# A macaron decoder layer on one core: inputs handed over in the layout in which the kernel reads them

## The chip, the cores and the metric

One core of a Trainium2 chip runs the whole layer in one launch. The metric is the device time of one execution in microseconds (us); the figure of a kernel is the median over its runs. A profile is of one further execution, with its own time.

## The reference, cut to what matters

Input `x` is (1, 256, 2048) float32, all weights are float32, and there is one layer:

```python
x = x + 0.5 * swiglu(rms_norm(x, ffn1_norm), w1, w3, w2)       # (silu(x@w1) * (x@w3)) @ w2, width 5632
h = rms_norm(x, mix_norm); proj = h @ w_in                     # columns q|k, v, o, i, f, u (4104)
y = concat[ mLSTM heads (4, chunkwise, conv on q|k) | S5 groups (64 groups of 16 channels, state 64) ]
x = x + y @ w_out                                              # S5: states by B, scan, out by C, gelu, GLU
x = x + 0.5 * swiglu(rms_norm(x, ffn2_norm), ...)
out = rms_norm(x, final_norm)
```

In the S5 part, each group's states are read out by `real(states * C)`, with `C = c_re + i c_im` of shape (64, 16, 64), and `d_skip` is a factor per channel.

## The kernel before, in words

**Products in three parts.** TensorE gets float32 numbers as two float32r parts, `hi` and `lo`, and forms `xh*wh + xl*wh + xh*wl`. Each weight is used once. The weights come in *steps*: a step is two k-tiles of 128 rows by 512 columns, 512 KB. `fetch` (L151) issues the load on SP's queue (`wraw`, 4 buffers), ScalarE casts it to `whi` (L157), and VectorE subtracts to `wlo` (L159; 4 buffers each). `plan` (L107) lists all steps in the order of use, and `weights` (L143) keeps three steps fetched ahead. `step_tok` (L162) is one step of a product with tokens on rows: 8 matmuls with `whi`, then 4 with `wlo`, 512 columns each.

**Activations with channels on rows.** The left operand needs channels on the partitions. `x` is loaded with tokens on partitions in four pieces of 512 columns (`load_x`, L257), and `transpose_x` (L329) turns one piece by 8 transposes on TensorE (L341), from whose PSUM result ScalarE writes `xh` (times the norm's gain, L346) and VectorE `xl` (L351). The norm's factor per token (`rstd`) is applied after the product, from sums of squares of `x` (`sumsq`, L325).

**The start.** `start` (L189) is the first product (w1, columns 0 to 511, 8 steps, called M0 to M7 here). Its order on PE, ACT and DVE is written out by hand: piece 0 of `x` is turned, then weight steps and the turning of pieces 1 to 3 alternate, with the sums of squares behind steps 4 to 7. Dummy matmuls (`warm`, L308: 8 and then 4) stand ahead of the first product. All DMAs on SP stand in program order; on the other engines a planner orders what isn't written out by hand.

**Vectors.** Norm gains, conv weights and the like are rows of 128 in HBM. `ffn1_norm` is loaded first and turned on TensorE (L272); the other 96 rows come by seven DMAs on POOL's queue (L287), are turned at the 6th step behind the start (L294) and copied to `cols`.

**Background tasks.** While the first FFN runs, each step's end (`tick`, L83) lets tasks of `s5_params` (L508) go, at about 0.42 per step: parameters of the S5 part are loaded by POOL's queue and, for each of 8 blocks `j`, tables are built and written back to HBM (`spill`, L762). For C, both parts are loaded with channels on rows (`craw`, L538), masked to two groups on VectorE (`stage_c`, L718), turned by two transposes on TensorE (L734) and copied to `w2` by ScalarE, the second with a minus sign (L735, L736). `clam` (L740) and `kzero` (L750) read `w2`.

**The end.** `tail` (L415) does the last 512 columns in two halves of 256, with loads of its own (L427).

Of the kernel before, what the change touches and what calls it, by code (L numbers as in the profile page):

```python
# [8 lines left out]
F32 = mybir.dt.float32  # L9
F32R = mybir.dt.float32r  # L10
# [30 lines left out]
WARM = 8  # L41
MORE_WARM = 4
# [20 lines left out]
class _Layer:  # L63
# [87 lines left out]
    def fetch(self, name, k, kk, c0, n):  # L151
        nc = self.nc
        view = self.wview(name)
        raw = self.wraw.tile([P, KK * NC], F32, name="wraw")[:, :kk * n]
        nc.sync.dma_start(out=raw.rearrange("p (k n) -> p k n", n=n), in_=view[:, k:k + kk, c0:c0 + n])
        hi = self.whi.tile([P, KK * NC], F32R, name="whi")[:, :kk * n]
        nc.scalar.copy(hi, raw)  # L157
        lo = self.wlo.tile([P, KK * NC], F32R, name="wlo")[:, :kk * n]
        nc.vector.tensor_sub(lo, raw, hi.bitcast(F32))  # L159
        return hi.rearrange("p (k n) -> p k n", n=n), lo.rearrange("p (k n) -> p k n", n=n)  # L160
# [28 lines left out]
    def start(self, acc, view, gain):  # L189

        W = lambda i: self.weights(view, i * KK, KK, 0, NC)
        M = lambda i, w: self.step_tok(acc, self.xs, [(i * KK, 0), (i * KK + 1, 0)], w, NC, i == 0, i == 7)
        T = lambda c, halves=(0, 1): self.transpose_x(c, gain, halves)
        ET = mybir.EngineType
        with self.tc.manual_schedule(engines={ET.PE, ET.Activation, ET.DVE}):
            self.load_x(0)
            T(0, (0,))
            self.ahead.append((self.steps[0], self.fetch(*self.steps.pop(0))))
            T(0, (1,))
            self.warm(MORE_WARM)  # L200
            self.ahead.append((self.steps[0], self.fetch(*self.steps.pop(0))))
            self.load_x(1)
            for i in range(8):
                M(i, W(i))
                if i % 2 == 0 and i < 6:
                    T(i // 2 + 1)
                if i % 2 == 0 and i < 4:
                    self.load_x(i // 2 + 2)
                if i >= 4:
                    self.sumsq(i - 4)  # L210
        self.finish_rstd()
# [22 lines left out]
    def wview(self, name):  # L234
        return self.a[name][0].rearrange("(k p) n -> p k n", p=P)


    def setup(self):
# [16 lines left out]
        vec0 = self.s5p.tile([KD, P], F32, name="vec0", tag="s5k0")  # L255
        nc.sync.dma_start(out=vec0, in_=self.a["ffn1_norm"][0].rearrange("(k p) -> k p", p=P))
# [13 lines left out]
        self.cols0 = c.tile([P, KD], F32, name="cols0")  # L270
        b = self.bank()
        nc.tensor.transpose(b[:, :KD], vec0, self.ident[:KD, :KD])  # L272
        nc.vector.tensor_copy(self.cols0, b[:, :KD])
        rows = 16 + 16 + 32 + 8 * 4
        vecs = self.s5p.tile([rows, P], F32, name="vecs", tag="s5k0")
        r = 0
        where = {}
        for name, n in (("mix_norm", 16), ("ffn2_norm", 16), ("conv_w", 32), ("conv_b", 8), ("mlstm_norm", 8),
                        ("d_skip", 8), ("b_glu", 8)):
            src = self.a[name][0]  # L280
            if name == "conv_w":
                src = src.rearrange("w (j p) -> (w j) p", p=P)
            elif name == "d_skip":
                src = src.rearrange("(j r) h -> j (r h)", r=8)
            else:
                src = src.rearrange("(k p) -> k p", p=P)
            nc.gpsimd.dma_start(out=vecs[r:r + n, :], in_=src)  # L287
            where[name] = r
            r += n
        self.cols = c.tile([P, rows], F32, name="cols")  # L290

        def late():
            b = self.bank()
            nc.tensor.transpose(b[:, :rows], vecs, self.ident[:rows, :rows])  # L294
            nc.vector.tensor_copy(self.cols, b[:, :rows])
            w = where["b_glu"]
            nc.vector.tensor_scalar(self.cols[:, w:w + 8], self.cols[:, w:w + 8], 0.5, None, op0=ALU.mult)
            w = where["mlstm_norm"]
            nc.vector.tensor_scalar(self.cols[:, w:w + 8], self.cols[:, w:w + 8], 0.5, None, op0=ALU.mult)
# [3 lines left out]
        nc.vector.memset(self.gcol, 0.0)  # L303
        for i, name in enumerate(("b_i", "b_f")):
            nc.gpsimd.dma_start(out=self.gcol[32 * i:32 * i + H, :], in_=self.a[name][0].rearrange("(h o) -> h o", o=1))
# [62 lines left out]
    def ffn(self, l, chunk_done):  # L368
        nc = self.nc
        w1, w3, w2 = (f"ffn{l}_{n}" for n in ("w1", "w3", "w2"))  # L370
        with ExitStack() as ctx:
# [4 lines left out]
            for hi_, n in enumerate(HALVES):  # L376
                gs = []
                self.rate = self.ffn1_rate if l == 1 else 1
                for c in range(n):
                    cc = c0 + c  # L380
                    ks = [(k, k) for k in range(KD)]
                    p1 = self.pair()
                    if l == 1 and cc == 0:
                        self.start(p1, w1, lambda k: self.cols0[:, k:k + 1])
                    else:
                        self.gemm_tok(p1, self.xs, w1, ks, cc * NC, NC)
                    s = []
                    for t in range(TT):
                        s.append(fp.tile([P, NC], F32, name=f"s{t}"))
                        nc.scalar.activation(s[t], p1[t], AF.Silu, scale=self.rstd[:, t:t + 1])  # L390
# [24 lines left out]
    def tail(self, w2, gs, c0):  # L415
# [6 lines left out]
        for half in range(2):  # L422
            col = c * NC + half * W
            ws = []
            for i, k0 in enumerate(range(0, n, 4)):
                raw = self.wraw.tile([P, KK * NC], F32, name="wraw")
                nc.sync.dma_start(out=raw.rearrange("p (k n) -> p k n", n=W),  # L427
                                  in_=self.wview(w2)[:, c0 * 4 + k0:c0 * 4 + k0 + 4, col:col + W])
# [79 lines left out]
    def s5_params(self, ctx):  # L508
# [13 lines left out]
        craw = [sp.tile([P, NJ, 64], F32, name=f"craw{i}") for i in range(2)]  # L522
# [6 lines left out]
        load(out=self.wgr, in_=self.wview("w_in")[:, :, GATE0:GATE0 + 2 * H])  # L529
# [7 lines left out]
        for i, nm in enumerate(("c_re", "c_im")):  # L537
            load(out=craw[i], in_=self.a[nm][0].rearrange("(j r) h p -> (r h) j p", r=8))  # L538
# [4 lines left out]
        maskg = sp.tile([P, 2], F32, name="maskg")  # L543
        maskq = sp.tile([P, 4], F32, name="maskq")

        def layout():
# [11 lines left out]
            V.tensor_reduce(maskg, self.ident.rearrange("p (q g h) -> p g q h", q=4, g=2), op=ALU.add, axis=AX.XY)  # L558
# [130 lines left out]
        def per_j(j):  # L689
# [26 lines left out]
            stc = [st.tile([P, 2, 64], F32, name=f"stc{ri}") for ri in range(2)]  # L716
# [520 lines left out]
```

## Time and profile before

| | |
|---|---|
| median of 3 runs | 1839.52 us (1839.28 to 1840.48) |
| the profiled execution | 1839.91 us, its span 1838.2 us |
| PE (TensorE) busy | 1821.5 us, 99% |
| DVE (VectorE) busy | 1064.4 us, 58% |
| ACT (ScalarE) busy | 818.1 us, 45% |
| POOL (GpSimd) busy | 348.9 us, 19% |
| read from HBM | 344.6 MB, mean 195 GB/s with all else |

Busy time of an engine is what its instructions cover. Matmuls overlap each other in the records, so the step from one start to the next tells more than a duration. "Idle before" is the time that an engine stood before an instruction, with what ended it.

### The profile page before, as it was taken

Reading aid. Unit: us, or ns where it says so; the run is one execution under the profiler, and the core shown is the slowest. Engines: PE = TensorE matmul, PEld = TensorE weight load, DVE = VectorE, ACT = ScalarE, POOL = GpSimd, SP = SyncE. Lnnn points to the kernel's source line nnn. Section 1 sums busy time; section 2 is a strip of 40 time slices with the busy share of each in tenths; the row PEclk is TensorE's granted clock in tenths of the full one; section 3 lists DMA queues with packets and bytes.
Section 4 is the critical chain, followed back from the end, with each engine's and each line's share of the span. In section 5 each row is a group of like instructions: output and inputs, shape, how many; then the busy total and the mean of one; then the engine's idle time right before and its main releaser. Section 6 shows DMA issues by size and latency. Waiting matters only on the chain.

```text
span 1838.2 us, 24018 instructions
## 1 busy us (share of the span) xinstructions
PE 1821.5 (99%) x9174; PEld 1527.0 (83%) x9174; DVE 1064.4 (58%) x1261; ACT 818.1 (45%) x982; POOL 348.9 (19%) x519
## 2 busy tenths in 40 slices
PE   9999999999999999999999999999999999999998
PEld 7888888888888888998977988888888888888887
DVE  5546855555555555578888665454544545454554
ACT  6444444334444445444454564444443334444343
POOL 4000799920000000065545100000000000000011
PEclk9999999999999999999999999999999999999999
DMA  8666676676666665767784556666665666666563
GB/s 275 196 186 185 192 217 214 213 242 196 196 197 195 188 198 195 198 181 208 184 211 149 190 189 201 193 192 189 189 187 192 193 194 191 189 193 186 193 193 128
DMA packets 185652, 358.26 MB, mean 195 GB/s; under 512 B 12064, under 2 KB 18336, under 8 KB 185408
## 3 DMA queue, kind: packets, MB, share of 16 engines
q1 hardware_dynamic: 181344, 344.51, 63.1%
q0 software_dynamic: 4048, 11.16, 1.7%
q8 instruction: 72, 1.18, 0.3%
q10 hardware_dynamic: 144, 1.05, 0.1%
q14 instruction: 44, 0.36, 0.1%
HBM read 344.61 MB, written 11.01 MB: 193 GB/s over the span
## 4 chain that ended last, share of the span: by engine, by line
PE 95%; DVE 2%; DMA 2%; issue 1%; ACT 0%; ACTq 0%; POOLq 0%; POOL 0%; SPq 0%; DVEq 0%
PE accb L177 84%; PE accb L225 2%; PE accb L231 2%; PE accb L226 2%; DVE wlo L159 1%; PE tpb L492 1%; DMA wraw<-in_w_in_dram 1%; PE tpb L341 0%; DMA wraw<-in_ffn_w_dram 0%; PE tpb L852 0%; PE accb L482 0%; PE accb L481 0%; PE accb L480 0%; PE tpb L891 0%; PE tpb L928 0%
## 5 line engine op out<-in xcount | busy, mean ns | idle before, releaser
L159 DVE TENSOR_TENSOR wlo<-wraw,whi 128x1024 fp32r<-128x1024 f32 x622 | 791.1, 1274 | 677.4 <-ACT whi L157 676.8
L157 ACT CAST whi<-wraw 128x1024 fp32r<-128x1024 f32 x622 | 654.4, 1053 | 885.3 <-PE accb L177 814.4
L177 PE MATMUL accb<-whi,xh 128*128 128x512 f32 x1536 | 603.5, 393 | 0.6 <-ACT whi L157 0.6
L177 PE MATMUL accb<-whi,xl 128*128 128x512 f32 x1536 | 598.9, 390 | 0.8 <-DVE xl L351 0.8
L177 PE MATMUL accb<-wlo,xh 128*128 128x512 f32 x1536 | 410.7, 389 | 0.0
L177 PEld LDWEIGHTS accb<-whi,xh 128*128 128x128 f32 x1536 | 289.0, 188 | 61.6 <-ACT whi L157 1.3
L177 PEld LDWEIGHTS accb<-whi,xl 128*128 128x128 f32 x1536 | 289.0, 188 | 60.3 <-DVE xl L351 1.6
L177 PEld LDWEIGHTS accb<-wlo,xh 128*128 128x128 f32 x1536 | 288.3, 188 | 60.1
L177 PE MATMUL accb<-whi,gh 128*128 128x512 f32 x664 | 259.8, 391 | 0.0
L177 PE MATMUL accb<-whi,gl 128*128 128x512 f32 x664 | 258.4, 389 | 0.0
L177 PE MATMUL accb<-wlo,gh 128*128 128x512 f32 x664 | 177.5, 389 | 0.0
L177 PEld LDWEIGHTS accb<-wlo,gh 128*128 128x128 f32 x664 | 124.6, 188 | 25.9
L177 PEld LDWEIGHTS accb<-whi,gh 128*128 128x128 f32 x664 | 124.6, 188 | 25.6
L177 PEld LDWEIGHTS accb<-whi,gl 128*128 128x128 f32 x664 | 124.7, 188 | 25.5
L1201 POOL TENSOR_TENSOR x<-x,fn 128x512 f32<-128x512 f32 x6 | 12.1, 2041 | 689.9 <-ACT junk L323 689.9
L703 POOL TENSOR_TENSOR tr<-s5rot,sp 128x128 f32<-128x128 f32 (+6 forms) x112 | 55.5, 496 | 160.2 <-DVE sp L643 156.7
L225 PE MATMUL accb<-xh,whi 128*128 128x256 f32 x256 | 63.5, 286 | 0.0
L226 PE MATMUL accb<-xl,whi 128*128 128x256 f32 x256 | 62.8, 283 | 0.0
L705 POOL TENSOR_TENSOR s5rot<-tr,tr 128x128 f32<-128x128 f32 (+6 forms) x112 | 61.0, 557 | 3.3
L704 POOL TENSOR_TENSOR tr<-s5rot,sp 128x128 f32<-128x128 f32 (+6 forms) x112 | 57.2, 511 | 0.0
L764 POOL DMA_DIRECT2D spillw<-s5w x16 | 8.6, 541 | 249.6 <-ACT s5w L735 239.2
L225 PEld LDWEIGHTS accb<-xh,whi 128*128 128x128 f32 x256 | 49.1, 192 | 0.8 <-issue 0.4
(316 smaller groups left out, 1345.5 us busy)
## 6 DMA issues: line engine op xcount, KB each, us to landing
wraw<-in_ffn_w_dram SPq DMA_DIRECT2D x528, 512.0 KB, 3.8
wraw<-in_w_in_dram SPq DMA_DIRECT2D x64, 512.0 KB, 5.7
wraw<-in_w_out_dram SPq DMA_DIRECT2D x32, 512.0 KB, 4.2
spillrot<-s5rot POOLq DMA_DIRECT2D x8, 512.0 KB, 5.4
spillw<-s5w POOLq DMA_DIRECT2D x16, 256.0 KB, 4.6
s5rot<-spillrot SPq DMA_DIRECT2D x8, 512.0 KB, 6.9
s5w<-spillw SPq DMA_DIRECT2D x16, 256.0 KB, 7.1
wraw<-in_w_glu_dram SPq DMA_DIRECT2D x8, 512.0 KB, 3.7
```

Of the source, the lines that this page charges most:

```text
L157: nc.scalar.copy(hi, raw)
L159: nc.vector.tensor_sub(lo, raw, hi.bitcast(F32))
L177: nc.tensor.matmul(acc[t][:, :n], lhsT=x, rhs=wt, start=first and t not in seen, stop=last and t not in left)
L225: nc.tensor.matmul(o(nt), lhsT=wh[:, kk, ns(nt)], rhs=xh, start=st, stop=False, **kw)
L226: nc.tensor.matmul(o(nt), lhsT=wh[:, kk, ns(nt)], rhs=xl, start=False, stop=False, **kw)
L231: nc.tensor.matmul(o(nt), lhsT=wl[:, kk, ns(nt)], rhs=xh, start=False, stop=sp, **kw)
L492: nc.tensor.transpose(b[:, o:o + P], s[t][:, kt * P:(kt + 1) * P], self.ident)
L703: G.tensor_tensor(tr[0][:, :, :k], rv[:, 0, :, 0:k], u0, op=ALU.mult)
L704: G.tensor_tensor(tr[1][:, :, :k], rv[:, 1, :, 0:k], u1, op=ALU.mult)
L705: G.tensor_tensor(rv[:, a, :, k:2 * k], tr[0][:, :, :k], tr[1][:, :, :k], op=op)
L764: nc.gpsimd.dma_start(out=d, in_=t)
L1201: nc.gpsimd.tensor_tensor(self.x[c][:, t, :], self.x[c][:, t, :], self.fn[:, c * NC:(c + 1) * NC], op=ALU.mult)
```

## The change

Host-side `_layout` hands the inputs over in other layouts; the kernel's arithmetic stays the same.

- `xT`: x with channels on rows (128 x 16 x 256), beside `x` itself. `start` loads `xT` in place of `x` and splits it straight from SBUF with 256-column instructions; the 32 transposes of L341 in the start go. `x` is loaded at steps 4 to 7; its sums of squares move to the ticks of the second product, and the first Silu (L390) runs at that product's 4th tick.
- `cols`: all 112 vectors with channels on rows in one DMA, the first on SP's queue. The transposes L272 and L294 and POOL's seven loads go; `gcol` is one load in place of two.
- `cT`: C turned and masked on the host. `stage_c` becomes two DMAs on POOL's queue per block straight into `w2`; the mask, the two transposes (L734) and the copy L735 go; the minus sign is a ScalarE instruction in place.
- Weights: every step lies in HBM as one block, 4 KB for each partition, instead of two rows of 2 KB (tail: one of 4 KB instead of four of 1 KB). The first step's load is cut into two DMAs, and its casts into two halves each.
- `warm` is 9 dummy matmuls once, instead of 8 and 4.

```diff
-WARM = 8
-MORE_WARM = 4
+WARM = 9
+    def load(self, name, k, kk, c0, n, parts=1):
+        raw = self.wraw.tile([P, KK * NC], F32, name="wraw")[:, :kk * n].rearrange("p (k n) -> p k n", n=n)
+        m = kk // parts
+        for i in range(0, kk, m):
+            self.nc.sync.dma_start(out=raw[:, i:i + m, :], in_=self.wview(name, k, c0)[:, i:i + m, :])
+        return raw
...
+        def split_x(k):
+            c, i = divmod(k, 4)
+            g = self.col("ffn1_norm", k)
+            nc.scalar.activation(self.xh[c][:, i, :], raw[c][:, i, :], AF.Copy, scale=g)
+            nc.vector.scalar_tensor_tensor(self.xl[c][:, i, :], raw[c][:, i, :], g, self.xh[c][:, i, :].bitcast(F32),
+                                           op0=ALU.mult, op1=ALU.subtract)
+        def prepare(i):
+            step, wr = w[i]
+            if i == 0:
+                tiles = self.split_tiles()
+                for kk in range(KK):
+                    split_x(kk)
+                    ready.append((step, self.split(wr, tiles, slice(kk, kk + 1))))
+                ready.pop()
+                return
+            if i < 8:
+                for kk in range(KK):
+                    split_x(i * KK + kk)
+            ready.append((step, self.split(wr)))
         with self.tc.manual_schedule(engines={ET.PE, ET.Activation, ET.DVE}):
-            self.load_x(0)
-            T(0, (0,))
-            self.ahead.append((self.steps[0], self.fetch(*self.steps.pop(0))))
...
+            load_xT(0, 0, 2)
+            load(0, KK)
+            load_xT(0, 2, 4)
+            load(1)
+            prepare(0)
+            load_xT(1)
+            load(2)
+            prepare(1)
+            load_xT(2)
+            load(3)
             for i in range(8):
-                M(i, W(i))
...
+                prepare(i + 2)
+                if i == 0:
+                    load_xT(3)
+                if i + 4 < 10:
+                    load(i + 4)
                 if i >= 4:
-                    self.sumsq(i - 4)
-        self.finish_rstd()
+                    self.load_x(i - 4)
+                self.step_tok(acc, self.xs, [(i * KK, 0), (i * KK + 1, 0)], ready.pop(0)[1], NC, i == 0, i == 7)
+        self.ahead = ready
...
             def stage_c():
                 for ri in range(2):
-                    src = craw[ri][:, j, :].unsqueeze(1).broadcast_to([P, 2, 64])
-                    self.tc.keep_in_program_order(V.tensor_tensor(
-                        stc[ri], src, maskg.unsqueeze(2).broadcast_to([P, 2, 64]), op=ALU.mult))
+                    nc.gpsimd.dma_start(out=w2[:, ri * P:(ri + 1) * P], in_=self.a["cT"][ri, :, j, :])
...
-                b2 = self.bank()
-                for ri in range(2):
-                    nc.tensor.transpose(b2[:, ri * P:(ri + 1) * P], stc[ri].rearrange("p g q -> p (g q)"), self.ident)
-                nc.scalar.copy(w2[:, 0:128], b2[:, 0:128])
-                nc.scalar.activation(w2[:, 128:256], b2[:, 128:256], AF.Copy, scale=-1.0)
+                nc.scalar.activation(w2[:, 128:256], w2[:, 128:256], AF.Copy, scale=-1.0)
```

## Rows read from the trace of the kernel before

**Rows 1.** The page: busy time and share of each engine

```profile
PE 1821.5 (99%) x9174; PEld 1527.0 (83%) x9174; DVE 1064.4 (58%) x1261; ACT 818.1 (45%) x982; POOL 348.9 (19%) x519
```

**Rows 2.** The page: chain of work that ended last, shares by engine

```profile
PE 95%; DVE 2%; DMA 2%; issue 1%; ACT 0%; ACTq 0%; POOLq 0%; POOL 0%; SPq 0%; DVEq 0%
```

**Rows 3.** Waits: engine, line, releaser, total us, times, longest us

```profile
PE tpb L991 <- DVE Dm L966: 2.6, 1, 2.6
PE accb L177 <- DVE hml L1030: 2.2, 1, 2.2
...
ACT whi L157 <- PE accb L177: 814.4, 517, 2.8
...
ACT whi L157 <- DMA wraw<-in_w_in_dram: 20.9, 12, 3.6
```

**Rows 4.** Timeline of PE: start us, duration us, line, tiles

```profile
1.52 3.59 PE L312 MATMUL tpb<-junk 128*128 128x512 bf16 x8 [1.52 <-DVE junk L260]
5.97 1.09 PE L341 MATMUL tpb<-ident,x 128*128 128x128 f32 x8 [0.69 <-DMA x<-in_x_dram]
...
8.49 0.50 PE L177 MATMUL accb<-whi,xh 128*128 128x512 f32 x1 [0.57 <-ACT whi L157]
...
22.96 0.50 PE L177 MATMUL accb<-whi,xl 128*128 128x512 f32 x1 [0.79 <-DVE xl L351]
...
25.59 1.03 PE L341 MATMUL tpb<-ident,x 128*128 128x128 f32 x8
26.38 0.48 PE L177 MATMUL accb<-whi,xh 128*128 128x512 f32 x1
...
34.63 0.39 PE L177 MATMUL accb<-whi,xh 128*128 128x512 f32 x1
...
37.35 0.39 PE L177 MATMUL accb<-whi,xh 128*128 128x512 f32 x1
...
50.96 0.25 PE L294 MATMUL tpb<-ident,vecs 96*128 96x96 f32 x1
50.99 0.48 PE L177 MATMUL accb<-whi,xh 128*128 128x512 f32 x1
```

**Rows 5.** Chain of waits in order of time: start us, duration us, what

```profile
1.25 4.67 DMA x<-in_x_dram
```

**Rows 6.** Timeline of ACT in the start

```profile
6.67 0.84 ACT L346 ACTIVATE xh<-tpb,cols 128x256 fp32r<-128x256 f32 x2 [4.37 <-PE tpb L341]
7.40 1.04 ACT L157 CAST whi<-wraw 128x1024 fp32r<-128x1024 f32 x1
...
11.38 1.04 ACT L157 CAST whi<-wraw 128x1024 fp32r<-128x1024 f32 x1 [1.26 <-DMA wraw<-in_ffn_w_dram]
12.64 1.05 ACT L157 CAST whi<-wraw 128x1024 fp32r<-128x1024 f32 x1 [0.21 <-DMA wraw<-in_ffn_w_dram]
```

**Rows 7.** Windows: stretch, length, busy of PE PEld DVE ACT POOL, PEclk, DMA, GB/s

```profile
0.00:5.00 5.00, 3.48 (x8) 1.03 (x8) 0.93 (x5) 1.49 (x2) 3.92 (x13) 1.00 0.48 120
5.00:12.00 7.00, 5.75 (x32) 4.31 (x32) 4.58 (x9) 4.07 (x7) 5.10 (x8) 1.00 1.04 394
12.00:18.00 6.00, 5.96 (x28) 4.62 (x27) 4.02 (x6) 2.95 (x6) 0.04 (x1) 1.00 1.04 281
18.00:26.00 8.00, 7.21 (x37) 5.66 (x36) 5.25 (x7) 5.67 (x8) 4.41 (x5) 1.00 0.96 322
26.00:36.00 10.00, 10.00 (x49) 8.35 (x48) 6.47 (x8) 9.68 (x22) 3.74 (x8) 1.00 0.88 243
36.00:44.00 8.00, 8.00 (x37) 6.64 (x36) 4.71 (x6) 6.41 (x9) 1.80 (x1) 1.00 0.81 275
950.00:955.00 5.00, 2.43 (x9) 1.56 (x8) 5.00 (x6) 1.75 (x3) 1.23 (x1) 0.90 1.01 255
955.00:960.00 5.00, 5.00 (x18) 3.88 (x16) 1.93 (x4) 2.34 (x7) 0.00 (x0) 0.76 0.91 295
```

**Rows 8.** Timeline of PE: the transposes of one S5 block

```profile
254.88 0.60 PE L730 MATMUL tpb<-ident,stg 128*128 128x128 f32 x4
255.32 0.38 PE L734 MATMUL tpb<-ident,stc 128*128 128x128 f32 x2
255.46 0.48 PE L177 MATMUL accb<-whi,xh 128*128 128x512 f32 x1
```

**Rows 9.** DMA issues: queue, count, KB each, median us from issue to landing

```profile
craw<-in_c_im_dram POOLq DMA_DIRECT2D x1, 256.0 KB, 6.0
```

More of the change, by code (lines that the diff above doesn't have):

```diff
@@ L149, in weights, with fetch, split_tiles, split @@
         return w
-    def fetch(self, name, k, kk, c0, n):
-        nc = self.nc
[L153 to L160, printed above, removed]
+    def fetch(self, *step):
+        return self.split(self.load(*step))
+    def load(self, name, k, kk, c0, n, parts=1):
[4 more added lines that the diff above has]
+        return raw
+    def split_tiles(self):
+        return (self.whi.tile([P, KK * NC], F32R, name="whi"), self.wlo.tile([P, KK * NC], F32R, name="wlo"))
+    def split(self, raw, tiles=None, ks=None):
+        nc = self.nc
+        kk, n = raw.shape[1:]
+        hi, lo = (t[:, :kk * n].rearrange("p (k n) -> p k n", n=n) for t in tiles or self.split_tiles())
+        ks = ks or slice(0, kk)
+        nc.scalar.copy(hi[:, ks, :], raw[:, ks, :])
+        nc.vector.tensor_sub(lo[:, ks, :], raw[:, ks, :], hi[:, ks, :].bitcast(F32))
+        return hi, lo
     def step_tok(self, acc, xs, part, w, n, first, last):
@@ L187, in gemm_tok, with start, load_xT, load @@
             self.tick()
[L189 to L193, printed above, removed]
+    def start(self, acc, gp):
+        nc = self.nc
         ET = mybir.EngineType
-        with self.tc.manual_schedule(engines={ET.PE, ET.Activation, ET.DVE}):
-            self.load_x(0)
-            T(0, (0,))
-            self.ahead.append((self.steps[0], self.fetch(*self.steps.pop(0))))
[L199 to L202, printed above, removed]
-            for i in range(8):
-                M(i, W(i))
[L205 to L208, printed above, removed]
+        raw = [gp.tile([P, 4, S], F32R, name="gl").bitcast(F32) for c in range(4)]
+        self.xh = [self.xTp.tile([P, 4, S], F32R, name=f"xh{c}") for c in range(4)]
+        self.xl = [self.xTp.tile([P, 4, S], F32R, name=f"xl{c}") for c in range(4)]
+        w, ready = {}, []
+        def load_xT(c, a=0, b=4):
+            nc.sync.dma_start(out=raw[c][:, a:b, :], in_=self.a["xT"][:, 4 * c + a:4 * c + b, :])
+        def load(i, parts=1):
+            w[i] = self.steps.pop(0)
+            w[i] = w[i], self.load(*w[i], parts=parts)
+        def split_x(k):
[17 more added lines that the diff above has]
+            ready.append((step, self.split(wr)))
+        with self.tc.manual_schedule(engines={ET.PE, ET.Activation, ET.DVE}):
+            load_xT(0, 0, 2)
[8 more added lines that the diff above has]
+            load(3)
+            for i in range(8):
+                prepare(i + 2)
[3 more added lines that the diff above has]
+                    load(i + 4)
@@ L254, in setup @@
         xin = self.a["x"][0].rearrange("(t p) n -> p t n", p=P)
-        vec0 = self.s5p.tile([KD, P], F32, name="vec0", tag="s5k0")
-        nc.sync.dma_start(out=vec0, in_=self.a["ffn1_norm"][0].rearrange("(k p) -> k p", p=P))
+        rows = sum(n for _, n in _COLS)
+        self.cols = c.tile([P, rows], F32, name="cols")
+        nc.sync.dma_start(out=self.cols, in_=self.a["cols"])
         self.load_x = lambda i, a=0, b=NC: nc.sync.dma_start(out=self.x[i][:, :, a:b],
@@ L269, in setup @@
         nc.vector.memset(self.mhalf, -0.5)
[L270 to L287, printed above, removed]
+        where, r = {}, 0
+        for name, n in _COLS:
             where[name] = r
             r += n
-        self.cols = c.tile([P, rows], F32, name="cols")
         def late():
[L293 to L299, printed above, removed]
+            for name in ("b_glu", "mlstm_norm"):
+                w = where[name]
+                nc.vector.tensor_scalar(self.cols[:, w:w + 8], self.cols[:, w:w + 8], 0.5, None, op0=ALU.mult)
         self.after(6, late)
@@ L302, in setup @@
         self.gcol = c.tile([GW, 1], F32, name="gcol")
-        nc.vector.memset(self.gcol, 0.0)
-        for i, name in enumerate(("b_i", "b_f")):
-            nc.gpsimd.dma_start(out=self.gcol[32 * i:32 * i + H, :], in_=self.a[name][0].rearrange("(h o) -> h o", o=1))
+        nc.gpsimd.dma_start(out=self.gcol, in_=self.a["gcol"])
         self.wgr = c.tile([P, KD, 2 * H], F32, name="wgr")
@@ L1227 @@
     arrays, args = {}, {}
-    for name in _INS:
-        v = _np.ascontiguousarray(inputs[name])
+    for name, v in _layout(inputs).items():
+        v = _np.ascontiguousarray(v)
         arrays[f"in_{name}_dram"] = v
```

61 lines of the change are left out of this document (46 added, 15 removed).

## The prediction, written before the change was run

> **What bounds the kernel now.** I read the page's busy shares first, then the chain of waits, then who waits for whom, and only then the places that the change touches. TensorE is busy 1821.5 of 1838.2 us [rows 1], and 95% of the chain that ends last is its own work [rows 2]. So only two kinds of time can be won: TensorE instructions that go away, and the few microseconds in which it stands. In mid-kernel it stands about 5 us, in the mixer, and both large waits there end on VectorE (2.6 and 2.2 us), not on a transfer [rows 3]. ScalarE's casts, which follow each weight load, wait 814.4 us for TensorE to free a buffer and only 20.9 us for the mixer's loads [rows 3]: weights normally arrive early. The remaining loss is at the front. The first real matmul starts at 8.49, and M8, the ninth weight step, at 34.63 [rows 4]. A step is 37.35 - 34.63 = 2.72 us, twelve matmuls of 0.227 [rows 4], so eight steps need 21.8 us, and 34.63 - 8.49 = 26.1 were used.
>
> **The start, transposes.** Three turnings of x stand in that stream (the first is ahead of it); the third takes 26.38 - 25.59 = 0.79 from its start to the next matmul [rows 4], so 2.4 of TensorE's work go; they are part of the 4.4 below, as the transfers decide how much of it is seen. The turning of the 96 vectors at 50.96 [rows 4] goes too: a transpose takes 0.79/8 = 0.10, so **0.1**.
>
> **The start, transfers.** These decide where the rest lands, so I count bytes. In the kernel before, 0.60 MB had moved by 5.0 (120 GB/s), then 394 GB/s to 12.0, when 3.36 MB had moved, then 281, 322, 243 and 275 GB/s in the next four stretches [rows 7]. The piece x0 landed at 1.25 + 4.67 = 5.92 [rows 5], when 0.96 MB had moved, though itself and what was ahead of it were 0.53. The load for the cast at 11.38 [rows 6] had 2.63 MB in and ahead of it, and 3.10 had moved; for the one at 12.64 it was 3.15 and 3.53. So a load lands when some 0.43 MB more than itself and its predecessors has moved. In the new order the sums are, in MB: cols 0.06, first half of xT0 0.32, first half of w0 0.58, second half of w0 0.84, w1 1.63, w2 2.68, w3 3.73, w4 4.78, w5 5.30, w8 6.87, then pieces of x between, so w9 7.92, w10 8.97, w11 10.02, w12 11.07.
> By that, half of w0 lands at 5 + (0.58 + 0.43 - 0.60)/0.394 = 6.04. ScalarE has split the first k-tile of xT by then (0.42, half of the 0.84 of two such instructions [rows 6]) and casts half a step, 0.55 of the 1.04 [rows 6]: M0 starts at 6.65 instead of 8.49. VectorE's parts, 0.44 and 0.66 by the same halving, end in time for matmuls 2 and 9. M0 ends at 9.4. w1 lands at 8.71, its cast ends at 9.8, a wait of 0.4: M1 runs to 12.55. w2 lands at 11.37, cast 12.47: no wait, M2 runs to 15.27. From here two bounds. If the queue keeps 394 GB/s, w3 lands at 14.0 and w4 at 16.7, M4 starts at 18.0 with no further wait and M8 at 28.9: 5.7 us gained. If the rates stay those of before at the same times, w3 lands at 14.85 (M3 at 15.95), w4 at 18.5 (M4 at 19.6, waited 0.9), M8 starts at 30.5, and the extra 2.1 MB of x between w8 and w12 bring w12 to 41.3, M12 starts at 42.4 where it was 34.63 + 4 x 2.72 = 45.5: 3.1 gained. I take the middle, **4.4**, because the parameter loads on POOL's queue that stood beside those stretches still run, but the channel-vector loads and the strided gate columns are gone from them. ScalarE keeps up: from M8 on it has a cast of 1.05 and two squares a step, as it had before.
>
> **S5's C.** Two of six transposes of each block go. The six take 255.46 - 254.88 = 0.58 from start to the next matmul, so two are 0.19 to 0.22 [rows 8]; times 8 blocks 1.5 to **1.75**. I take 1.75, as each is a 0.11 slot in a stream that never stands there. The copy on ScalarE and the masks on VectorE go too and cost or give nothing: ScalarE is idle half the time behind TensorE [rows 1, 3]. The new waits: the minus sign on ScalarE, `clam` on VectorE and `kzero` on TensorE now wait for a DMA from POOL's queue. Behind the waiting ScalarE instruction stand the weight casts. A load of that queue took 6.0 us to land [rows 9]; the task that issues it is two tasks, about 4.8 steps or 13 us, ahead of the one that uses it, and a cast runs some 9.1 us ahead of its matmul (three steps and four matmuls), so 8.0 us of lateness are hidden beyond that. I cost it at 0; without that cover it is the slower rival below.
>
> **Weights in 4 KB pieces.** In the FFNs nothing waits for a load, so 0; it is hidden behind three steps of look-ahead. In the mixer I bound it from a gain of 2.6 + 2.2 = 4.8 us (both waits vanish [rows 3]) to a loss of the same size (both double), and take 0, since both end on VectorE. The tail stream has no wait on loads either: 0.
> The Trainium skill ("DMA: Bandwidth & Descriptors", section "Rules for kernel authors") asks for at least 1 MiB per transfer and gives a fixed 2.0 us beside bytes/436 GB/s for one DMA, which speaks against halving the first loads; the trace differs, as queued pieces of 512 KB moved at 394 GB/s [rows 7]. By the rule, five early pieces one after another would cost an estimated 10 us of fixed time.
>
> **Sum.** 4.4 + 0.1 + 1.75 = 6.3. The profiled execution took 1839.91, its span 1838.2 and 1.7 around it; that is 0.4 over the median 1839.52. So 1839.9 - 6.3 = 1833.6 on that execution and **1833.2** as a median.
>
> **Rivals.**
> 1. *The doubled read of x eats the start.* If all stretches from 12 on move only 243 GB/s [rows 7], w4 lands at 19.6, w10 at 36.9, w12 at 45.5 and M12 starts at 46.6, 1.1 later than before. The sum is then 1.75 + 0.1 - 1.1 = 0.8: 1838.7. For it: transfers were saturated (DMA 1.04) at only 281 GB/s in 12 to 18 [rows 7]. Against it: in 26 to 44 the share is 0.88 and 0.81, so these rates are partly what was asked for.
> 2. *The clock falls in a gap of the start.* Behind a stand of 2.6 us in the mixer the granted clock is 0.90 and then 0.76 of full in two stretches of 5 us [rows 7], part of the time at 1.2 GHz, 0.5 + 1.2 = 1.7 us lost. The dummies, nine at 0.44 [rows 4], end near 5.5, and M0 comes at 6.65: 1.1 of standing, against 0.9 between 5.1 and 5.97 before [rows 4]. One loss of 1.7 gives 1834.9. The Trainium skill ("TensorE: Matmul & The Clock Gate", section "Part 1: The HAM clock gate") says that throttled is the default state and activity releases it; the mixer's rows agree.
> 3. *Slower: C's loads hold the casts.* If POOL is so far behind (its queue is in order, with tables and write-backs ahead) that ScalarE stands 12 us at each block's minus sign, TensorE loses 12 - 8.0 = 4 us in each of 8 blocks, 32 in all: 1865. It turns slower than before once a stand passes 8.0 + 6.3/8 = 8.8 us. Against it: the issue stands 13 us ahead of the use and lands in 6 [rows 9].
> 4. *Small first pieces pay a fixed price each.* Of x0's 4.67 us [rows 5] its bytes explain 0.52/0.394 = 1.3 [rows 7]; if the other 3.3 were paid again for each of the two pieces more, w1 and all behind it come 6.6 later: 1839.8. Against it: the casts at 11.38 and 12.64 waited for two loads that landed 1.3 apart [rows 6]. The Trainium skill's rule above points this way.
> 5. *Better.* The start takes its fast bound and the mixer's waits halve: 5.7 + 1.9 + 2.4 = 10.0, 1829.5.
>
> **How the numbers follow.** Forecast 0.60, rivals in order 0.12, 0.07, 0.05, 0.04 and 0.12. The likeliest's own range is 1830.5 to 1835.5 (start 5.7 to 3.1, mixer within 1). For 8 in 10 I reach down to rival 5's neighbourhood and up past rivals 2 to half of 1: 1829.0 to 1837.0. A measurement tells 0.2% (3.7 us, so below 1835.8 or above 1843.2) from no change. Faster holds the forecast (nearly all), rivals 2 and 5: 0.76. Same holds rivals 1 and 4 and a little of the forecast's upper end: 0.18. Slower is rival 3 and a little for a mixer that reorders badly: 0.06.
>
> **What would show it.** In the changed profile M0 should start at 6.2 to 7.0 and M8 at 29 to 30.5; no L341 in the start; each S5 block should have four transposes on TensorE and no stand of ScalarE before the minus sign; from M12 to the mixer the distance should be shorter by 1.75 and nothing else; the mixer's stands should remain near 5 us and end on VectorE. I am wrong if M12 is later than 44, if the minus sign waits for a DMA beyond 8 us, or if the time between the start and the mixer changes by more than the transposes.

## The result and the profile after

The changed kernel takes **1891.02 us** (median of 4 runs, 1890.36 to 1891.91); the kernel before took 1839.57 in the runs beside it (1839.28 to 1840.48). The ratio is 1.0279, 95% interval 1.0261 to 1.0297. Forecast were 1833.2 and a range of 1829 to 1837: the time lies 54 us above the range, on the side given to rival 3. The profiled execution took 1891.91, its span is 1890.2, so 52.0 more than before.

The page of the changed kernel, engines' busy time and the chain that ended last, to be held against [rows 1, 2]:

```profile
PE 1814.4 (96%) x9121; PEld 1519.2 (80%) x9121; DVE 1054.9 (56%) x1242; ACT 817.9 (43%) x975; POOL 320.7 (17%) x525
...
PE 86%; POOL 8%; DVE 3%; issue 1%; ACT 1%; DMA 1%; SPq 0%; POOLq 0%; ACTq 0%; DVEq 0%
```

TensorE does 7 us less work in 53 matmuls fewer: 50 transposes and 3 dummies. But POOL, which stood at 0% of the chain, now has 8%. The waits (engine, line, releaser; total us, times, longest us), to be held against [rows 3]:

```profile
ACT s5w L754 <- DMA s5w<-in_cT_dram: 75.9, 7, 65.9
DVE tw L761 <- DMA s5w<-in_cT_dram: 70.9, 6, 66.3
PE accb L187 <- DVE wlo L169: 57.4, 1, 57.4
```

One stand of 57.4 us is more than the whole loss. What ended it is read from three timelines (start us, duration us, engine, line, tiles, in brackets the idle time before and its releaser; `x2` at the end is two instructions in one row). ScalarE:

```profile
268.22 1.06 ACT L168 CAST whi<-wraw 128x1024 fp32r<-128x1024 f32 x1 [2.17 <-PE accb L187]
335.18 0.31 ACT L754 ACTIVATE s5w<-s5w 128x128 f32<-128x128 f32 x1 [65.90 <-DMA s5w<-in_cT_dram]
335.39 2.92 ACT L168 CAST whi<-wraw 128x1024 fp32r<-128x1024 f32 x3
```

VectorE, and then POOL:

```profile
334.97 0.29 DVE L761 TENSOR_TENSOR tw<-s5w,sp 128x128 f32<-128x128 f32 x1 [66.26 <-DMA s5w<-in_cT_dram]
```

```profile
330.72 0.59 POOL L782 DMA_DIRECT2D spillrot<-s5rot  x1 [0.30 <-POOL s5rot L731]
331.31 0.54 POOL L782 DMA_DIRECT2D spillw<-s5w  x1
331.85 1.09 POOL L744 DMA_DIRECT2D s5w<-in_cT_dram  x2
```

ScalarE finishes a cast at 269.3 and then stands 65.9 us at the minus sign (L754) with the next casts queued behind it; VectorE stands 66.3 us at `clam`'s first product (L761). TensorE lives 8 us on weights already split and stops. C's load, which all wait for, is issued at 331.85, because POOL was busy with tables until then, and lands 3 us later: it was not slow, it was issued late. Whose C this is, the order in the trace tells. Each block has one sign (L754) and, just ahead of it in the program text, one copy of its transposed B (L753), and both run in the order of the blocks. ScalarE, besides the sign at 335.18 shown above:

```profile
29.49 0.31 ACT L754 ACTIVATE s5w<-s5w 128x128 f32<-128x128 f32 x1 [2.94 <-DMA s5w<-in_cT_dram]
...
30.64 0.31 ACT L754 ACTIVATE s5w<-s5w 128x128 f32<-128x128 f32 x1
...
244.10 0.59 ACT L753 COPY s5w<-tpb 128x512 f32<-128x512 f32 x1 [0.29 <-PE tpb L752]
...
373.08 0.59 ACT L753 COPY s5w<-tpb 128x512 f32<-128x512 f32 x1 [0.30 <-PE tpb L752]
...
439.37 0.59 ACT L753 COPY s5w<-tpb 128x512 f32<-128x512 f32 x1 [0.30 <-PE tpb L752]
```

So the sign at 335.18 is the third, that of block 2 (the blocks count from 0). It stands behind block 0's copy (244.10) and ahead of block 1's (373.08), while its own block's copy is the one at 439.37; the signs of blocks 0 and 1 were moved up even into the start. On POOL, C's load at 331.85 is the third pair too (the first two were issued at 22.59 and 23.75), and the write-backs of all eight tables stand ahead of it (count; ns min/median/max; first and last start):

```profile
L782 POOL DMA_DIRECT2D spillrot<-s5rot x8: 582/598/622, 228.7 to 330.7; - x8
```

So the load stands behind the table work of all eight blocks. Before the change the sign needed TensorE's transposes and could not run ahead of them.

In the stand the granted clock falls; windows (stretch, length, TensorE busy, PEclk, DMA share, GB/s):

```profile
250.00:277.00 27.00, 27.00 (x134) 1.00 0.55 179
277.00:300.00 23.00, 2.06 (x10) 0.60 0.14 59
...
320.00:336.00 16.00, 0.00 (x0) 0.50 0.21 78
336.00:346.00 10.00, 9.54 (x40) 0.83 0.79 265
```

The start of the changed kernel, TensorE, against [rows 4], and two windows of it, against [rows 7]:

```profile
6.10 0.50 PE L187 MATMUL accb<-whi,xh 128*128 128x512 f32 x1 [0.77 <-ACT whi L168]
...
31.85 0.39 PE L187 MATMUL accb<-whi,xh 128*128 128x512 f32 x1
...
38.64 0.50 PE L187 MATMUL accb<-whi,xh 128*128 128x512 f32 x1 [1.19 <-ACT whi L168]
42.16 0.50 PE L187 MATMUL accb<-whi,xh 128*128 128x512 f32 x1 [0.48 <-ACT whi L168]
...
45.03 0.39 PE L187 MATMUL accb<-whi,xh 128*128 128x512 f32 x1
```

```profile
5.00:12.00 7.00, 4.51 (x18) 2.84 (x17) 4.24 (x8) 3.88 (x7) 2.30 (x3) 1.00 1.00 311
12.00:18.00 6.00, 4.76 (x21) 3.61 (x20) 3.61 (x8) 4.04 (x7) 2.63 (x3) 1.00 1.02 397
```

M0 comes 2.4 us earlier than before and M8 (31.85) 2.8, but M12 (45.03) only 0.5: most of the head start is given back.

To see where each part of the change acts I use two marks in the profiles: the first matmul that reads `dg` (the mixer begins) and the first that reads `hsh` (S5's output projection). All values from the profiled executions, in us:

| kernel | to `dg` | `dg` to `hsh` | `hsh` to the end | span |
|---|---|---|---|---|
| before | 775.0 | 278.4 | 784.8 | 1838.2 |
| after | 832.1 | 272.6 | 785.5 | 1890.2 |
| weights alone | 773.5 | 272.2 | 784.9 | 1830.6 |
| C alone, users pinned | 773.4 | 279.6 | 784.8 | 1837.8 |
| after, C as before | 775.5 | 273.1 | 785.5 | 1834.1 |
| after, users pinned | 772.5 | 272.1 | 785.6 | 1830.2 |
| the same, old start | 771.8 | 272.8 | 784.9 | 1829.5 |
| B laid out, loads in order | 770.1 | 273.6 | 785.5 | 1829.2 |

So the changed kernel lost 57.1 ahead of the mixer, won 5.8 in it and lost 0.7 behind it: 52.0.

### The profile page after: what moved, and what is told of

It is laid out like the page before. It is cut to its first block, busy times and chain, and to the rows that moved or that the text cites. A ratio compares the mean times of both kernels' runs of the same rounds, so it can differ in the third digit from the quotient of the medians.

```text
span 1890.2 us, 23910 instructions
## 1 busy us (share of the span) xinstructions
PE 1814.4 (96%) x9121; PEld 1519.2 (80%) x9121; DVE 1054.9 (56%) x1242; ACT 817.9 (43%) x975; POOL 320.7 (17%) x525
## 3 DMA queue, kind: packets, MB, share of 16 engines
q8 instruction: 71, 1.16, 0.2%
## 4 chain that ended last, share of the span: by engine, by line
PE 86%; POOL 8%; DVE 3%; issue 1%; ACT 1%; DMA 1%; SPq 0%; POOLq 0%; ACTq 0%; DVEq 0%
PE accb L187 76%; POOL tr L729 3%; POOL s5rot L731 2%; POOL tr L730 2%; PE accb L270 2%; PE accb L276 2%; PE accb L271 2%; DVE wlo L169 1%; PE tpb L523 1%; DMA wraw<-in_ffn_w_dram 1%; ACT whi L168 0%; PE tpb L870 0%; PE accb L513 0%; PE accb L512 0%; PE accb L511 0%
## 5 line engine op out<-in xcount | busy, mean ns | idle before, releaser
L169 DVE TENSOR_TENSOR wlo<-wraw,whi 128x1024 fp32r<-128x1024 f32 (+1 forms) x623 | 788.3, 1268 | 663.6 <-ACT whi L168 663.5
L168 ACT CAST whi<-wraw 128x1024 fp32r<-128x1024 f32 (+1 forms) x623 | 653.9, 1052 | 861.6 <-PE accb L187 793.5
L187 PE MATMUL accb<-wlo,xh 128*128 128x512 f32 x1536 | 412.0, 390 | 57.4 <-DVE wlo L169 57.4
L187 PEld LDWEIGHTS accb<-whi,gl 128*128 128x128 f32 x664 | 125.0, 188 | 25.6
L729 POOL TENSOR_TENSOR tr<-s5rot,sp 128x4 f32<-128x4 f32 (+6 forms) x112 | 50.6, 452 | 146.9 <-DVE sp L669 143.8
L271 PEld LDWEIGHTS accb<-xl,whi 128*128 128x128 f32 x256 | 49.1, 192 | 0.1
L731 POOL TENSOR_TENSOR s5rot<-tr,tr 128x4 f32<-128x4 f32 (+6 forms) x112 | 47.4, 435 | 3.0
```

Of the source, the lines that this page charges most:

```text
L168: nc.scalar.copy(hi[:, ks, :], raw[:, ks, :])
L169: nc.vector.tensor_sub(lo[:, ks, :], raw[:, ks, :], hi[:, ks, :].bitcast(F32))
L187: nc.tensor.matmul(acc[t][:, :n], lhsT=x, rhs=wt, start=first and t not in seen, stop=last and t not in left)
L271: nc.tensor.matmul(o(nt), lhsT=wh[:, kk, ns(nt)], rhs=xl, start=False, stop=False, **kw)
L729: G.tensor_tensor(tr[0][:, :, :k], rv[:, 0, :, 0:k], u0, op=ALU.mult)
L731: G.tensor_tensor(rv[:, a, :, k:2 * k], tr[0][:, :, :k], tr[1][:, :, :k], op=op)
```

## The experiments

The theory: one meeting of two queues that both run in order. The planner moved block 2's two users of C (the sign and `clam`) up to block 0, while C's load stands on POOL behind the tables. Its rivals: C's load is slow for itself; the weights' layout or the start costs the time; the hoist alone is the fault. Medians and ratios are against runs of the kernel before on the same chip (1839.06, 1839.29 and 1839.40 us in the three groups of four; the first group ran on another chip than the other two, so across groups the ratios compare better than the times).

**C as before** in the changed kernel (early load, mask, two transposes):

```diff
-    nc.gpsimd.dma_start(out=w2[:, ri * P:(ri + 1) * P], in_=self.a["cT"][ri, :, j, :])
+    V.tensor_tensor(stc[ri], craw..., maskg..., op=ALU.mult)
...
+    nc.tensor.transpose(b2[:, ri * P:(ri + 1) * P], stc[ri]..., self.ident)
```

> The changed kernel with S5's C alone handed over as before (one early load, mask on VectorE, two transposes a block on TensorE); the start, the vectors and the weights' layout stay changed. Theory: the whole loss is one stand of 57.4 us at block 2, where ScalarE's minus sign and VectorE's products come up while C's load for that block still stands on POOL's queue behind the tables. Then the stand goes, and its 2 us of low clock, while the two transposes of each block come back: 1891.0 - 57.4 - 2.0 + 1.75 = 1833.4, between 1831 and 1836. Rival, the new weight layout or the new start costs the time: over 1880.

Measured 1835.60, ratio 0.9981 (0.9972 to 0.9990). The stand is gone: C's hand-over is the cause. It is 2.2 above the expectation's middle; in its profile a fall of the clock in the start, shown below, takes 1.7.

**The weights' layout alone**, on the kernel before:

```diff
-    in_=view[:, k:k + kk, c0:c0 + n]
+    in_=self.wview(name, k, c0)      # self.a[name][c, k // KK]
```

> The kernel before with the weights' new layout alone (4 KB in one piece for each partition of a step, gate columns and last columns packed too). From the first first-FFN transposes to the first gated matmul of the S5 half, the mixer took 278.4 us before and 272.6 after. Theory: that gain of 5.8 belongs to the layout, as the mixer's loads land sooner and its stand and low clock shrink: 1839.5 - 5.8 = 1833.7, between 1832 and 1836. Rival: the mixer's gain comes from C or from another order of the planner: 1839 to 1840. Rival, the layout causes the loss: over 1880.

Measured 1832.54, ratio 0.9964 (0.9951 to 0.9976), as the theory had it: the layout is worth 6.5 us; in its profile, which is 7.6 shorter, 6.2 are won in the mixer and 1.5 ahead of it. The mixer's waits in its profile, TensorE's and then ScalarE's for the mixer's loads:

```profile
PE accb L176 <- DVE hml L1030: 1.2, 2, 0.9
PE accb L176 <- ACT hmh L1029: 1.1, 1, 1.1
PE tpb L991 <- ACT whi L156: 0.4, 1, 0.4
```

```profile
ACT whi L156 <- DMA wraw<-in_w_in_dram: 5.8, 5, 2.5
```

Before, ScalarE's casts stood 20.9 us for these loads and TensorE 2.6 and 2.2 us [rows 3], each time with a low clock behind it: behind the first stand the two stretches in [rows 7], behind the second these two of the kernel before (columns as in [rows 7]).

```profile
975.00:980.00 5.00, 3.71 (x11) 2.79 (x12) 4.22 (x7) 3.11 (x6) 4.84 (x3) 0.79 0.55 162
980.00:985.00 5.00, 5.00 (x21) 4.16 (x20) 4.26 (x6) 3.43 (x11) 3.14 (x3) 0.87 0.72 274
```

With the new layout the clock is 1.00 in every stretch of 10 us from 940 to 1000. TensorE's waits in the mixer shrink from 5.0 to 2.7 us in all, and the four stretches at a low clock had lost 3.4 by their own column, which makes 5.7 of the 6.2. The sum is good to 1 or 2 us: another stretch, from 790 to 830, reads 0.96 in the kernel before and 1.00 here.

**C's new hand-over alone**, on the kernel before:

```diff
-    load(out=craw[i], ...)           # and mask, two transposes, copy
+    nc.gpsimd.dma_start(out=w2[:, ri * P:(ri + 1) * P], in_=self.a["cT"][ri, :, j, :])
```

> The kernel before with C's new hand-over alone. Theory: the same meeting of the hoisted minus sign of block 2 and C's load behind the tables, as both orders stand there too (C's third load is number 390 on POOL, the sign the first but one of ScalarE's S5 work): a stand of 57 us, with 2 us of clock and 1.75 won: 1839.5 + 57.4 + 2.0 - 1.75 = 1897, between 1885 and 1905. Rival, the stand needs the new start, which shifts POOL's and ScalarE's work against each other: 1838 to 1845.

Measured 1912.40, ratio 1.0396 (1.0382 to 1.0410): the theory's stand is there with 57.3, and a second that I had not expected. TensorE's waits, and ScalarE in the start:

```profile
PE accb L177 <- DVE wlo L159: 57.8, 2, 57.3
PE accb L177 <- ACT xh L346: 10.6, 1, 10.6
```

```profile
32.41 0.31 ACT L723 ACTIVATE s5w<-s5w 128x128 f32<-128x128 f32 x1 [10.68 <-DMA s5w<-in_cT_dram]
32.62 1.55 ACT L346 ACTIVATE xh<-tpb,cols 128x256 fp32r<-128x256 f32 x4
```

Here the planner put a sign ahead of the start's own split of x. Of the 15 us by which the expectation missed, 10.6 are this same mechanism at a second place.

**The users pinned**: both held in program order on their engines, C's loads left on POOL behind the tables.

```diff
-    nc.scalar.activation(w2[:, 128:256], w2[:, 128:256], AF.Copy, scale=-1.0)
+    self.tc.keep_in_program_order(nc.scalar.activation(
+        w2[:, 128:256], w2[:, 128:256], AF.Copy, scale=-1.0))
...
-    V.tensor_tensor(tw[0], w[:, 0], lr_, op=ALU.mult)
+    self.tc.keep_in_program_order(V.tensor_tensor(tw[0], w[:, 0], lr_, op=ALU.mult))
```

> The changed kernel with the two users of C, ScalarE's minus sign and VectorE's first product, held in program order on their engines; C's loads stay on POOL's queue behind the tables. Theory: it is the hoist that meets the late load. Block 2's users then come up near 244 + 2 x 66 = 376 us, when the tables, done at 374 in the kernel before, have let C's load go: no stand, or one under 8 us that is hidden. ScalarE's 2.9 us stand before the sign of block 0 in the start goes too, and with it the waits of 1.2 and 0.5 us of M10 and M11: 1891.0 - 59.4 - 1.5 = 1830, between 1828 and 1835. Rival, C's load is slow or late for itself wherever its users stand: 1880 to 1891. Rival in between: the tables end 20 us after the use: 1840 to 1850.

Measured 1832.58, ratio 0.9964 (0.9950 to 0.9977). Two lines of order take 58 us away. POOL's issue for block 2 and ScalarE at block 2:

```profile
365.64 1.09 POOL L744 DMA_DIRECT2D s5w<-in_cT_dram  x2 [5.81 <-PE accb L187]
```

```profile
379.70 0.59 ACT L753 COPY s5w<-tpb 128x512 f32<-128x512 f32 x1 [0.30 <-PE tpb L752]
380.19 0.32 ACT L754 ACTIVATE s5w<-s5w 128x128 f32<-128x128 f32 x1
```

The load is even later than in the changed kernel (365.6 against 331.9), but its user comes at 380.2 instead of 269.3.

**Shorter tables**: the last doubling of each table replaced by a fill, users hoisted as in the changed kernel.

```diff
-    lambda: table(6, 7), spill]
+    lambda: G.memset(rv[:, :, :, 64:128], 0.0), spill]
```

> The changed kernel with the last doubling of each table left out (six products of 64 columns a pair are replaced by one fill with zeros, so the upper half of every table is wrong). Theory: the stand of block 2 lasts as long as POOL still has tables ahead of C's load; the left-out instructions took 35.8 us in all before the load's issue, the eight fills some 3: the load goes 33 us earlier, the stand shrinks from 57.4 to about 25 and the time to 1858, between 1850 and 1865. Rival, the load itself is slow or held by the write-back of block 0: the stand keeps 50 us or more, 1884 to 1891.

Measured 1866.28, ratio 1.0147 (1.0133 to 1.0161). The stand shrank from 57.4 to 31.8, and with POOL's issue, now at 305.44, the sign came at 308.78:

```profile
305.44 1.09 POOL L744 DMA_DIRECT2D s5w<-in_cT_dram  x2
```

```profile
308.78 0.31 ACT L754 ACTIVATE s5w<-s5w 128x128 f32<-128x128 f32 x1 [40.27 <-DMA spillk<-s5k]
```

The trace names a write-back (`spillk`) as the releaser, but POOL issued that at 306.53, behind C's load, and VectorE's product of the same block, at 308.58, is put down to C's load. So the tables set the length: the issue comes 26.4 us earlier and the stand is 25.6 shorter. It is not 32 shorter, and the time lies 1 us outside my bounds. I had counted all 35.8 us of the left-out products, but only 30 of the 48, 19.4 us, ran in the stand. The 18 ahead of it, 16.4 us, were slow (last section), and the tables that move up into their place would have run fast in the stand; this reading was not tested by itself.

**C loaded whole and early**, into tiles of its own, ScalarE copying each block's half; nothing pinned.

```diff
-    nc.gpsimd.dma_start(out=w2[:, ri * P:(ri + 1) * P], in_=self.a["cT"][ri, :, j, :])
+    load(out=ct[i], in_=self.a["cT"][i])             # once, early
...
+    nc.scalar.copy(w2[:, 0:128], ct[0][:, j, :])
+    nc.scalar.activation(w2[:, 128:256], ct[1][:, j, :], AF.Copy, scale=-1.0)
```

> The changed kernel with C loaded whole, once, early, into two tiles of its own (4 KB for each partition) from which ScalarE copies each block's half; nothing is pinned, and ScalarE's copies for block 2 still stand hoisted behind block 0's. Theory: the hoist alone does no harm where the data is there; the copies now wait only for the write-back of block 0, which POOL issues ahead of the later tables (it was issued at 275.9 in the changed kernel, where ScalarE came up at 269.3): a stand of 8 us or less, hidden: 1832 to 1836. Rival, the hoist itself is the fault, whatever it waits for: a stand of over 30 us, 1865 or more.

Measured 1840.77, 1838.8 to 1846.9, ratio 1.0014 (1.0004 to 1.0024): between theory and rival. The data is there, but the hoisted copy now stands for the next late thing, the write-back of block 0 that frees its buffer, issued by POOL at 288.04:

```profile
290.46 0.30 ACT L753 COPY s5w<-ct 128x128 f32<-128x128 f32 x1 [15.27 <-DMA spillw<-s5w]
```

15.3 us instead of my 8, of which TensorE felt 8.7. So the hoist by itself does harm as well, by how late POOL is with whatever the hoisted instruction waits for.

**C alone with its users pinned**, on the kernel before:

```diff
+    nc.gpsimd.dma_start(out=w2[:, ri * P:(ri + 1) * P], in_=self.a["cT"][ri, :, j, :])
+    self.tc.keep_in_program_order(...)      # the sign, clam's first product
```

> The kernel before with C's new hand-over alone and its two users held in program order. Theory: both stands of the run with C alone (57.3 us at block 2 and 10.6 in the start, before the first x, where ScalarE's signs of blocks 0 and 1 stood ahead of the casts) are the hoist's, and what is left is the two transposes a block: 1839.2 - 1.75 = 1837.5, between 1836.5 and 1838.5. Rival, C's transposes were no part of the end: 1839.2. Rival, the late load still meets its use: over 1841.

Measured 1839.15, ratio 0.9997 (0.9988 to 1.0006). Both stands are gone, so both were the hoist's. But the 1.75 do not reach the end: the mixer begins 1.6 us earlier and takes 1.2 longer. Its waits of TensorE in the mixer:

```profile
PE tpb L979 <- DVE Dm L954: 2.6, 1, 2.6
PE accb L177 <- DVE hml L1018: 2.5, 2, 2.2
PE tpb L952 <- DVE oth L988: 1.2, 1, 1.2
```

`oth` was 0.2 in the kernel before. I read it as the same late stretch of the mixer, reached earlier and standing longer; no run isolates this.

**The start.** The new start was next: is it worth its 4.4?

**The old start**, with the weights' layout and C pinned:

```diff
-    self.start(p1, gp)
+    self.start(p1, w1, lambda k: self.cols0[:, k:k + 1])     # x0 transposed on TensorE
```

> The kernel before with the weights' layout (1832.5) and C handed over with its users pinned, but with the old start and the vectors as before. Theory: the new start by itself wins nothing as it stands, so this is the weights' run less C's 1.75 us of transposes: 1830.8, between 1829.5 and 1832, better than the changed kernel with the users pinned (1832.6). Rival, the new start is worth its 4.4 us and another thing takes them in that run: 1834 to 1837 here.

Measured 1832.33, ratio 0.9963 (0.9951 to 0.9976), against 1832.58 with the new start: by itself the new start wins nothing that these runs can tell; 4.4 us they would have shown. (The expectation's 1830.8 was missed by 1.5, 0.3 beyond its range: C's transposes are hardly seen here either.) What held it up:

**B laid out**, so that its two loads come in pieces of 2 KB instead of eight loads in pieces of 64 B; users pinned.

```diff
-    for q in range(4):
-        load(out=braw[i][:, 8 * q:8 * q + 8, :], in_=src[:, 8 * q:8 * q + 8, :])
+    load(out=braw[i], in_=self.a["bT"][i])
```

> The kernel with the users pinned (1832.6) and, besides, S5's B handed over laid out: two loads in pieces of 2 KB for each partition in place of eight in pieces of 64 B. Theory: those small pieces, which POOL now issues at 4.6 us where nine small vector loads held them back to 10.2 before, are what takes the start's rate in 5 to 12 us down to 306 GB/s from 401 in the kernel with the new layout and the old start. With them gone it is near 400 again, some 0.65 MB more has moved by 12, the waits of M1, M2 and M4 (1.0, 1.3 and 1.2) shrink by 2 to 3: 1830, between 1828.5 and 1831. Rival, the start is bound by the order and number of its own bytes: 1832 to 1833.

Measured 1831.05, ratio 0.9953 (0.9940 to 0.9967), 1.5 better than without by the medians; the two spread over 1829.4 to 1832.3 and 1831.9 to 1833.5, so the times alone don't settle it. Windows of the kernel with users pinned, then of this one (busy of PE, PEld, DVE, ACT and POOL, clock, DMA share, GB/s):

```profile
5.00:12.00 7.00, 4.97 (x20) 3.15 (x19) 4.57 (x8) 3.89 (x8) 2.29 (x3) 1.00 1.02 306
```

```profile
5.00:12.00 7.00, 4.04 (x15) 2.74 (x16) 4.10 (x8) 4.24 (x8) 3.09 (x10) 1.00 1.00 357
```

At about the same DMA share the rate rises from 306 to 357, half of the way to the 401 expected. What held the other half back is open.

**B laid out, and the start's loads in order of use**: x's third piece behind w3, its fourth behind w5.

```diff
-    load_xT(2)
     load(3)
+    load_xT(2)
...
-    if i == 0:
-        load_xT(3)
     if i + 4 < 10:
         load(i + 4)
+    if i == 1:
+        load_xT(3)
```

> The kernel of the run with B laid out, and the start's loads in the order of use: the third piece of x behind w3 and the fourth behind w5, in place of ahead of w3 and w4. Theory: w3 and w4 land 512 KB, 1.3 us, sooner, M4's wait of 1.2 us goes if it is still there: 0.5 to 1.2 better than with B laid out alone, 1829, between 1827.5 and 1830.5. Rival, B's layout has already removed the waits: no difference of more than 0.4.

Measured **1829.84** (1829.12 to 1830.93), ratio 0.9949 (0.9936 to 0.9961): the best version, 9.5 us under the kernel before and 61 under the changed one. M4's wait (1.16 us with the users pinned) is absent from its timeline, but it is absent with B laid out alone too, as the rival had it. The step from B alone is 1.2, and the two ranges overlap, so a gain of the order by itself is not shown. Together with B's layout it is 2.7 under the 1832.58 of the users pinned; those ranges are apart, the intervals of the two ratios overlap.

**Eleven dummies** on top of that, and **eleven dummies with C early and pinned** (the edit of C loaded whole, above):

```diff
-WARM = 9
+WARM = 11
```

> The kernel with B laid out and the start's loads in order of use (1829.8), with eleven dummies ahead of the first matmul in place of nine. Theory: in its profile the first matmul came 0.6 us after the dummies and took the time of half the clock (0.79 for 0.50), and M0 took 4.7 us in place of 2.7; two more dummies of 0.44 close that gap, so runs without the fall become the rule: 1829.1, between 1828 and 1830, and a narrower spread. Rival, the fall has nothing to do with the gap, or the dummies hold M0 up by 0.2: 1829.8 to 1830.3.

> The kernel of the run with eleven dummies, and C loaded whole and early into tiles of its own, its users pinned. Theory: with the users pinned no stand is left for C to take away, and ScalarE's extra copy of 0.3 us a block lies beside TensorE: no difference of more than 0.7 from the run with eleven dummies, 1828.5 to 1830. Rival, the late loads of C on POOL's queue still cost something unseen: 1 us or more better. Rival, 1 MB of C early slows the start: 1830 to 1832.

Measured 1830.57 (1828.77 to 1831.73) and 1831.89 (1830.80 to 1833.32). The dummies made no difference that these runs tell, and the spread grew from 1.8 to 3.0 us instead of narrowing: three of the five runs still have a mean clock of 0.996 or 0.997 (1830.6 to 1831.7 us), the other two 0.999 (1828.8 and 1829.9). C early was no better, by the medians 1.3 worse, with overlapping ranges. Neither is a reason to change the best version.

## Why the prediction was wrong, step by step

All three of its signs of being wrong came: M12 started at 45.03, the minus sign waited 65.9 us, and the way from M12 to the mixer grew by 57.6 us (787.1 from 729.5).

**C's new waits, costed at 0: the step that failed.** It said that the task that issues C's load "is two tasks, about 4.8 steps or 13 us, ahead of the one that uses it". That is the order of the program text. The planner changes the order on ScalarE, VectorE and POOL, and the distance turned from 13 us ahead to 62.6 behind (331.85 - 269.3). Rival 3 named this mechanism and POOL's in-order queue as its place, at 5%, but as eight stands of 12; it came as one of 65.9 at the block whose sign was hoisted into the table work. The six other waits of ScalarE for C are 10.0 in all (75.9 - 65.9): one of 2.9 in the start, ahead of all tables, and five of 1.0 to 2.3 behind block 2, when POOL had none left. The argument against it, that the load lands in 6, was true (3 here) and beside the point. TensorE's part also bears out the cover: 65.9 - 57.4 = 8.5 against the 8.0 worked out.

**The start, 4.4.** M0 came at 6.10 for 6.65, but M8 at 31.85 for 28.9 to 30.5 and M12 at 45.03 for at most 42.4; at the end these runs show nothing left of it (1832.58 against 1832.33 with the old start). What failed is "the channel-vector loads and the strided gate columns are gone": nine such small loads stand ahead of B's on POOL, which issues B's first at 10.23 in the kernel with the weights alone; with one of the nine left, B's 64 B pieces were issued from 4.58, into the very stretch that the estimate ran at 394 GB/s, and 311 came. With B laid out 357 came (306 with the users pinned), so B's pieces account for about half of what was missing. On top, in the changed kernel, ScalarE stood 2.9 us for the hoisted sign of block 0, which came back as the waits of 38.64 and 42.16; with the users pinned only 0.24 us of them is left. With B laid out and the loads in order the time is 2.5 under the old start's (1832.33, same chip). What B's layout would give the old start was not run, so how much of the 2.5 belongs to the new start is open. The first halved loads cost little, as the sum had it and rival 4 had not.

**C's transposes, 1.75.** Right up to the mixer (1.6 by the marks), wrong at the end (0.25): the prediction had them on a path that does not stand, but the mixer behind them does.

**Weights in 4 KB pieces, 0 within 4.8.** Measured -6.5, the largest gain of the change, outside the bounds. "Both end on VectorE" was the misreading: the last engine of a wait was taken for its cause, though ScalarE's 20.9 us for the mixer's loads stood in the same group [rows 3]. With them at 5.8, `Dm`'s wait went from 2.6 to 0.4 (now ended by ScalarE) and `hml`'s longest from 2.2 to 0.9. The low clock behind the two stands went with them, some 3.4 us, and was not in the bounds, though rival 2 had priced it at 1.7 for one of them. By which link a late load delays `Dm` was not isolated.

**Rival 2** was real in some executions, though not the decider: see the last section. In the changed kernel's own profile the clock in the start is 1.00. **Sum.** Without the hoist the change gives 1832.58, inside the forecast's 1830.5 to 1835.5, but by other terms than those it added up; that agreement is luck.

Open: in every kernel with the new start the stretch behind `hsh` is 0.6 us or more longer (785.5 or 785.6, once 786.3, against 784.8 or 784.9). The cause was not looked for.

## What to carry to other kernels

Where a scheduler writes the order, a new wait must be checked in its order, on every engine that takes part: ask which instruction can now move up, and what stands ahead of its data on the issuing queue. A load that replaces computed data removes the dependency that kept its users in place; pin the users, or load it ahead of that queue's work. And a small load that is removed from a queue lets the next one go earlier, so look at what comes next.

## What the hardware showed that I had not expected

A product on POOL that meets VectorE's split of the weights takes longer. Three products of a table in the changed kernel, all of one shape: between two splits, on top of one, and in the stand.

```profile
225.88 0.61 POOL L729 TENSOR_TENSOR tr<-s5rot,sp 128x256 f32<-128x256 f32 x1
...
227.14 1.59 POOL L730 TENSOR_TENSOR tr<-s5rot,sp 128x256 f32<-128x256 f32 x1
...
329.01 0.61 POOL L730 TENSOR_TENSOR tr<-s5rot,sp 128x256 f32<-128x256 f32 x1
```

VectorE's split that the second one met, 1.63 us where it takes 1.22 by itself:

```profile
226.63 1.63 DVE L169 TENSOR_TENSOR wlo<-wraw,whi 128x1024 fp32r<-128x1024 f32 x1 [1.19 <-ACT whi L168]
```

The 18 products of this size ahead of the stand took 0.91 us in the mean, the 30 in it 0.65. So a backlog that is measured beside work (tables ended at 374 in the kernel before) drains faster once all stand (at 331 here). The Trainium skill ("SBUF — State Buffer", section "Who interferes with whom") says that a VectorE instruction with two inputs in SBUF contends with a POOL instruction that reads SBUF, over a pair of ports that is an exclusive lock. The rows agree: the split reads two tiles in SBUF, and 0.61 behind the 1.12 us for which it still ran would be 1.73, against the 1.59 measured.

The clock also falls in short gaps of the start, in some executions. With C as before, TensorE stood 1.30 us ahead of M0 and 1.02 inside it; the windows behind:

```profile
9.00:10.00 1.00, 0.92 (x2) 0.53 1.06 392
10.00:11.00 1.00, 1.00 (x4) 0.50 1.07 272
11.00:12.00 1.00, 1.00 (x4) 0.50 1.05 234
```

0.50 is 1.2 GHz: with a part of the stretch from 12 to 13, about 3.5 us at that level, 1.7 lost, the size that rival 2 gave. In the kernel with the users pinned, stands of 0.96 to 1.32 us ahead of M0, M1 and M2 left the clock at 1.00. In the best version's profile M0's matmuls follow each other at 0.43 us instead of 0.23 with the clock column at 1.00 throughout. It is the spacing of the stretches at 0.50 above, so I read it as the lower level, which the column did not show:

```profile
6.19 0.79 PE L187 MATMUL accb<-whi,xh 128*128 128x512 f32 x1 [0.64 <-ACT whi L168]
6.78 0.63 PE L187 MATMUL accb<-whi,xl 128*128 128x512 f32 x1
7.21 0.63 PE L187 MATMUL accb<-whi,xh 128*128 128x512 f32 x1
```
